# A new first stage, new visits to the caches and a re-dealt last norm in a one-layer inference step

## The chip, the cores and the metric

The kernel runs on one core of a Trainium2 chip. The core has TensorE (PE, matrix multiplies; PEld is its weight load), VectorE (DVE), ScalarE (ACT), GpSimd (POOL) and SyncE (SP), which here only issues DMAs. Data lie in HBM, in the on-chip SBUF of 128 partitions, and in PSUM, which PE accumulates into and which DVE and ACT read. The metric is the device time in microseconds of one execution; the number compared is the median over several executions.

## The reference

One layer of a decoder trunk is computed for a prompt of 256 positions and for 8 samples of 4 new positions, together 288 tokens of width 2048, all in float32:

```python
z = x @ w_in                                   # h, Bg, Cg, q, k, v, g_a, g_b
ya = gate_b * causal_dwconv3(gate_c * h)       # mixer A
# mixer B: three head groups with windows (128, 512, 2048) and dilations (1, 4, 16),
# 4 heads of 128 each, ALiBi; the softmax is merged over the groups
mixed = sigmoid(g_a) * (ya @ w_branch_a) + sigmoid(g_b) * (yb @ w_branch_b)
x1 = layernorm(ALPHA * x + mixed @ w_out)
a, b = split(x1 @ w_up)
y = layernorm(ALPHA * x1 + (silu(causal_dwconv3(a)) * b) @ w_down)
```

The samples attend to cached keys and values (`cache_kv0`, `cache_kv1`, `cache_kv2`). Beside `y` the outputs are the window buffers: new keys and values, the caches with the new rows behind them, and the last rows entering the two convolutions. So the cache tiles that the attention reads are also written out again.

## The kernel before, in words

Tokens are columns and features are rows. x lies as 16 chunks (`KD`) of 128 features by 288 tokens. Each float32 operand of a large product is split in two: a copy rounded to the type `fp32r` (ACT, `whi`, `xh`) and the remainder (DVE, `wlo`, `xl`). A block of 128 output features takes, for each of its 16 chunks, three matmuls of 288 columns: `whi` by `xh`, `whi` by `xl`, `wlo` by `xh` (`mms`, L217 to L219). `product` (L196) takes a prepared weight block, calls `prepare` for the next (one load of 1 MB on SP's queue, L176, and its split in halves by ACT and DVE, L223), and then issues the 48 matmuls. PE runs one product after another: 36 for q, k and v, 48 for mixer A, 64 for the two gated branches, 16 for `w_out`, then 88 for `w_up` and 48 for `w_down` in three parts.

**First stage.** While the data land, PE runs `N_WARM` matmuls on zeros (L235). The first three blocks of `w_in` are worked on together. `FIRST` (L69) cuts the 16 chunks into six pieces: 2, 2, 2, 2, 4 and 4 chunks. For each piece x comes by one DMA (L253; the first four from ACT's queue, the last two from SP's), two weight blocks by a second (`dd`, L254) and the third block by a third (`wst`, L255). ACT casts and DVE subtracts piece by piece: x (`xh`, `xl`), the two blocks (`yal`, `cache`), the third block (`whi`, `wlo`). PE (L285) goes by piece, then by the three terms, then by chunk and block. x lies in SBUF as two halves of 144 tokens per chunk with `HX` = 160 elements from half to half; one matmul reads the halves alternately. In the compiled program the DMAs of ACT's and SP's queues use eight completion semaphores in turn, so that a DMA is issued only when the eighth before it has landed.

**Visits to the caches.** The sample attention reads 18 key tiles and 18 value tiles of 1 MB. It is a generator, `sample_steps`, which `product` advances at a fixed rate (`N_STEP` of `N_STEP_BLOCKS`, L201 to L205), from the first k product on. At each step PE visits two tiles (L450 for keys, L506 for values, eight float32 matmuls of 512 columns a visit, or 32 of 128 in group 0), and `fetch_two` (L418) then loads the next two tiles into two `cache` buffers and writes them out again. Before each group DVE masks the queries, or the weights, by sample in one pass of 1024 columns (`by_batch`, L412). So there are 9 visits for the keys and 9 for the values. `prompt_attention` (L340 to L398) is spread over products in the same way.

**Last norm.** The last `w_down` products end in `dd`; `finish_out` (L712) normalises it. PE sums the last parts into mean and mean square (L686, L687). DVE and ACT work out the variance and its inverse root, with one correction step on DVE (L736, L737) whose result `dev` lies in PSUM. Each of 16 chunks of `dd` then needs the mean subtracted, the factor multiplied and gain and bias applied. `NORM_DVE` lists the passes of DVE in order ("m" subtract, "r" multiply, with first chunk and count); POOL subtracts chunks 8 to 15 (`MEAN_POOL`) and multiplies 12 to 15 (`OUT_POOL`), for which ACT copies the factor to SBUF (`r_pool`, L738). ACT applies gain and bias (L747) to chunks 0 to 7 and 12 to 15, DVE (L745) to 8 to 11. Six stores go out in `OUT_ORDER` (L748).

The order on each engine follows program order and explicit pairs (`behind`, `tc.issue_after`); a scheduler places the rest.

Of the kernel before, what the change touches and what calls it, by code (L numbers as in the profile page):

```python
# [11 lines left out]
F32R = mybir.dt.float32r  # L12
# [5 lines left out]
P = 128  # L18
# [11 lines left out]
HX = 160  # L30
# [23 lines left out]
C_M0 = C_TM + NT  # L54
C_M1 = C_M0 + NG * P
# [31 lines left out]
def layer_kernel(ctx: ExitStack, tc: tile.TileContext, ins, outs):  # L87
# [40 lines left out]
    spent = [0]  # L128
# [42 lines left out]
    def prepare():  # L171
        src, nk = next(w_left, (None, 0))
        if nk == 0:
            return
        st = sb(wp, [P, KD, P], "wst")
        d = sp.dma_start(st[:, :nk, :], src.rearrange("p (k c) -> p k c", c=P))  # L176
# [19 lines left out]
    def product(x):  # L196

        w = w_ready.pop(0)
        if not w_ready:
            prepare()  # L200
        if steps_on[0]:  # L201
            spent[0] += N_STEP
            while spent[0] >= N_STEP_BLOCKS:
                spent[0] -= N_STEP_BLOCKS
                next(steps, None)  # L205
# [31 lines left out]

    xh = sb(big, [P, KD, 2, HX], "xh", F32R)
    xl = sb(big, [P, KD, 2, HX], "xl", F32R)
# [6 lines left out]
    w_two_lo = [sb(wk, [P, 2, HK, P], "cache", F32R, bufs=2) for _ in range(2)]  # L246
# [4 lines left out]
    for k0, n, queue in FIRST:  # L251
        k = slice(k0, k0 + n)
        (act if queue == "act" else sp).dma_start(xs[:, k], x_in[:, k])  # L253
        sp.dma_start(w_two[:, :, k], w_in_two[:, :, k])  # L254
        sp.dma_start(w_one[:, k], w_in_one[:, k])  # L255
    splits = []
    for k0, n, _ in FIRST:
        k = slice(k0, k0 + n)
        splits.append(split(xh[:, k, :, :H], xl[:, k, :, :H], xs[:, k].rearrange("p k (a h) -> p k h a", h=2)))
        h = slice(k0 % HK, k0 % HK + n)  # L260
        splits.append(split(w_two_hi[:, :, k], w_two_lo[k0 // HK][:, :, h], w_two[:, :, k]))
        splits.append(split(w_one_hi[k0 // HK][:, h], w_one_lo[k0 // HK][:, h], w_one[:, k]))
    for before, after in zip(splits, splits[1:]):
        for i in range(2):
            behind(after[i], before[i])
# [3 lines left out]
    def first_three():  # L269
# [10 lines left out]
        for k0, n, _ in FIRST:  # L280
            for term in range(3):
                for k in range(k0, k0 + n):
                    xk = x[term == 1][:, k].rearrange("p h a -> p a h")
                    for b in range(3):
                        i = pe.matmul(  # L285
                            o[b], first_w(term == 2, b, k), xk, start=k == 0 and term == 0, stop=k == KD - 1 and term == 2
                        )
                        if before is not None:
                            behind(i, before)
                        before = i  # L290
        return [t.rearrange("p a h -> p h a") for t in o]

    cst = sb(big, [P, C_M0], "cst")

# [106 lines left out]
    bmask = cst[:, C_BM : C_BM + NB * NS].rearrange("p (b r) -> p b r", b=NB)  # L401
    tmask = cst[:, C_TM : C_TM + NT]

    sw = sb(wk, [P, NH * NB * NS + 1152], "sw", bufs=1)
    sw_m = sw[:, : NH * NB * NS].rearrange("p (j b r) -> p j b r", j=NH, b=NB)
    sw2 = sw[:, NH * NB * NS :]

    def by_batch(src):

        m = sw_m  # L410
        shape = [P, NH, NB, NS]
        dve.tensor_tensor(m, src.unsqueeze(2).broadcast_to(shape), bmask.unsqueeze(1).broadcast_to(shape), ALU.mult)  # L412
        return m

    cache_left = iter([(which, n) for which in ("ck", "cv") for n in range(N_CT)])
    cache_tiles = []

    def fetch_two():  # L418

        for _ in range(2):  # L420
            which, n = next(cache_left, (None, 0))
            if which:
                t = sb(wk, [P, 2048], "cache", bufs=2)
                behind(sp.dma_start(t, ins[which][n]), w_load[0])
                sp.dma_start(outs["o_" + which][n], t)
# [9 lines left out]
    def sample_steps():  # L435
        fetch_two()
        yield
        row = []
        s = sw2[:, :SW]
        sbias = cst[:, C_SB : C_SB + SW]  # L440
        for g in range(NG):
            qm = by_batch(q_s[:, g])
            cols = P if g == 0 else NT * P
            p = sb(ps, [P, cols], "long", bufs=1)
            for b in range(NB):
                if g > 0 or b % 4 == 0:
                    c = cache_tiles.pop(0)
                o = (b % 4) * NH * P if g == 0 else 0
                for j in range(NH):
                    row.append(pe.matmul(  # L450
                        p[j * NS : (j + 1) * NS], qm[:, j, b, :], c[:, o + j * cols : o + (j + 1) * cols],
                        start=b == 0, stop=b == NB - 1,
                    ))
                if g == NG - 1 and b == NB - 1:
# [9 lines left out]
                if b == NB - 1 or (g > 0 and b % 2 == 1):  # L464
                    in_a_row(row)
                    row = []
                    fetch_two()
                    yield
            sg = s[:, g * P : (g + 1) * P]
            if g == 0:  # L470
                dve.tensor_tensor(sg, p, sbias[:, :P], ALU.add)
            else:
                pick_t(sg, p, sbias[:, g * P : (g + 1) * P])
        dve.tensor_tensor(s[:, NG * P :], pn, sbias[:, NG * P :], ALU.add)
        st = sb(wk, [P, 4], "st", bufs=4)
        dve.reduce_max(st[:, 0:1], s, AX.X)
        dve.tensor_scalar_mul(st[:, 1:2], st[:, 0:1], -SCALE)
        act.activation(s, s, AF.Exp, bias=st[:, 1:2], scale=SCALE, accum_out=st[:, 2:3])
        dve.reciprocal(st[:, 3:4], st[:, 2:3])
        dve.tensor_scalar_mul(s, s, st[:, 3:4])  # L480
        pt = att()
        for g in range(NG):
            pe.transpose(pt[:, g * P : (g + 1) * P], s[:, g * P : (g + 1) * P], ident)
        pt2 = att()
        pe.transpose(pt2[: NG * NS, :P], s[:, NG * P :], ident)
        sT = sw2[:, : NG * P].rearrange("p (g r) -> p g r", g=NG)
        act.copy(sT, pt[:, : NG * P].rearrange("p (g r) -> p g r", g=NG))
        sTn = sw2[: NG * NS, NG * P : NG * P + P]
        act.copy(sTn, pt2[: NG * NS, :P])
        vn = sw2[: NG * NS, NG * P + P : NG * P + P + NH * P].rearrange("p (j d) -> p j d", j=NH)  # L490
        pv = att()
        for j in range(NH):
# [528 lines left out]
```

## Time and profile before

| | |
|---|---|
| median of 3 runs | 1757.73 us (1757.28 to 1758.61) |
| profiled execution | 1758.0 us, its span 1756.2 us |
| PE busy in the span | 1738.8 us |
| DVE, ACT, POOL busy | 1006.7, 797.9, 243.7 us |
| bytes moved | 436.25 MB, mean 248 GB/s |

How to read it: times in the trace count from the span's first instruction. A busy share is an average over stages, so the stage decides what a change is worth; the chain of work that ended last tells which instruction each piece of time belongs to. Rows of matmuls overlap: one of 288 columns is shown with 286 ns, but they start 0.12 us apart. A row of the timeline gives start, duration, engine, line, operation, result and operands, a count where rows are merged, and in brackets the idle time before it and what ended it. "x18" behind a row means 18 instructions.

### The profile page before, as it was taken

The page shows a single profiled execution, that of the slowest core. Times are in us where ns is not written, and L with a number is a line of the kernel's source. Part 1 is how long each engine was busy: PE and PEld are TensorE (multiplying, and loading weights), DVE is VectorE, ACT ScalarE, POOL GpSimd, SP SyncE. Part 2 cuts the span into 40 slices and gives each one's busy share as a digit, 9 for nine tenths or more (in the row PEclk, how much of TensorE's full clock was granted, in tenths as well). Part 3 has the DMA queues.
Part 4 walks back from the last instruction along what each step waited for, and adds up shares of the span by engine and source line. Part 5 has one row for each costly group of instructions (what it writes and reads, how often), then busy time and mean ns, then how long its engine had stood idle before and what let it go on. Part 6 is the DMA issues. An engine that isn't in the chain of part 4 may idle for free.

```text
span 1756.2 us, 33518 instructions
## 1 busy us (share of the span) xinstructions
PE 1738.8 (99%) x14257; PEld 1710.7 (97%) x14257; DVE 1006.7 (57%) x1278; ACT 797.9 (45%) x1142; POOL 243.7 (14%) x404
## 2 busy tenths in 40 slices
PE   9999999999999999999999999999999999999996
PEld 9999999999999999999999999999999999999996
DVE  5444445555555444455588888765555555555554
ACT  5444444334434333344455655544454443345444
POOL 0000000000000000001165333300011110011165
PEclk9999999999999999999999999999999999999998
DMA  9477787787787877477766656566666666666662
GB/s 330 170 287 274 274 307 283 280 326 282 299 322 272 319 300 264 150 252 264 259 251 224 231 219 231 224 226 230 224 232 221 235 218 238 219 236 217 225 217 102
DMA packets 61350, 436.25 MB, mean 248 GB/s; under 512 B 7312, under 2 KB 9360, under 8 KB 17296
## 3 DMA queue, kind: packets, MB, share of 16 engines
q1 hardware_dynamic: 59472, 429.40, 66.4%
q10 hardware_dynamic: 1728, 4.72, 0.7%
q8 instruction: 111, 1.82, 0.4%
q14 instruction: 39, 0.32, 0.1%
HBM read 389.89 MB, written 94.53 MB: 276 GB/s over the span
## 4 chain that ended last, share of the span: by engine, by line
PE 99%; DMA 0%; DVE 0%; ACT 0%; SPq 0%; ACTq 0%; issue 0%; DVEq 0%
PE acc L217 32%; PE acc L219 31%; PE acc L218 31%; PE long L506 1%; PE long L450 1%; PE acc L285 1%; DMA dd<-in_w_in 0%; PE att L391 0%; ACT yah L747 0%; DVE dd L723 0%; PE att L351 0%; PE acc L383 0%; PE att L349 0%; PE att L374 0%; PE att L687 0%; PE att L686 0%
## 5 line engine op out<-in xcount | busy, mean ns | idle before, releaser
L223 DVE TENSOR_TENSOR wlo<-wst,whi 128x1024 fp32r<-128x1024 f32 (+2 forms) x584 | 709.1, 1215 | 613.1 <-ACT whi L223 607.6
L223 ACT CAST whi<-wst 128x1024 fp32r<-128x1024 f32 (+2 forms) x584 | 593.3, 1017 | 888.0 <-PE acc L218 777.7
L217 PE MATMUL acc<-xh,whi 128*128 128x288 f32 (+1 forms) x3216 | 922.8, 287 | 0.0
L218 PE MATMUL acc<-xl,whi 128*128 128x288 f32 (+1 forms) x3216 | 920.4, 286 | 0.0
L219 PE MATMUL acc<-xh,wlo 128*128 128x288 f32 (+1 forms) x3216 | 920.3, 286 | 0.0
L217 PEld LDWEIGHTS acc<-xh,whi 128*128 128x128 f32 x3216 | 607.8, 189 | 10.3 <-ACT h L606 2.5
L218 PEld LDWEIGHTS acc<-xl,whi 128*128 128x128 f32 x3216 | 607.8, 189 | 0.2 <-issue 0.2
L219 PEld LDWEIGHTS acc<-xh,wlo 128*128 128x128 f32 x3216 | 607.8, 189 | 0.0
L217 PE MATMUL acc<-yah,whi 128*128 128x288 f32 x1216 | 347.9, 286 | 0.0
L219 PE MATMUL acc<-yah,wlo 128*128 128x288 f32 x1216 | 347.7, 286 | 0.0
L218 PE MATMUL acc<-yal,whi 128*128 128x288 f32 x1216 | 347.7, 286 | 0.0
L217 PEld LDWEIGHTS acc<-yah,whi 128*128 128x128 f32 x1216 | 229.7, 189 | 2.5 <-ACT h L628 2.5
L218 PEld LDWEIGHTS acc<-yal,whi 128*128 128x128 f32 x1216 | 229.8, 189 | 0.0
L219 PEld LDWEIGHTS acc<-yah,wlo 128*128 128x128 f32 x1216 | 229.8, 189 | 0.0
L584 POOL COPY qk_s<-u 128x2 f32<-128x2 f32 x44 | 38.1, 866 | 571.4 <-ACT u L798 448.6
L572 DVE SCALAR_TENSOR_TENSOR cy<-u,prm,cy 128x304 f32<-128x304 f32 x120 | 72.4, 603 | 3.8 <-ACT cy L570 0.7
L643 POOL TENSOR_TENSOR ya<-ya,dd 128x288 f32<-128x288 f32 x16 | 13.6, 850 | 306.0 <-DVE ya L642 306.0
L595 DVE TENSOR_TENSOR ya<-cy,acc 128x256 f32<-128x256 f32 x88 | 23.5, 310 | 33.8 <-PE acc L219 33.7
L223 ACT CAST yah<-ya 128x288 fp32r<-128x288 f32 x76 | 32.7, 430 | 16.6 <-DVE ya L600 8.5
L584 POOL COPY cm<-u 128x2 f32<-128x2 f32 x16 | 3.0, 185 | 256.5 <-DVE u L611 256.5
L677 POOL TENSOR_TENSOR cache<-cache,dd 128x288 f32<-128x288 f32 x29 | 29.1, 1002 | 52.6 <-DVE dd L763 33.6
L223 DVE TENSOR_TENSOR yal<-ya,yah 128x288 fp32r<-128x288 f32 x76 | 34.9, 460 | 1.3 <-ACT yah L223 1.1
(174 smaller groups left out, 830.2 us busy)
## 6 DMA issues: line engine op xcount, KB each, us to landing
wst<-in_w_in SPq DMA_DIRECT2D x113, 1024.0 KB, 6.2
wst<-in_w_up SPq DMA_DIRECT2D x88, 1024.0 KB, 4.8
wst<-in_w_down SPq DMA_DIRECT2D x32, 1024.0 KB, 4.8
cache<-in_ck SPq DMA_DIRECT2D x18, 1024.0 KB, 6.4
out_o_ck<-cache SPq DMA_DIRECT2D x18, 1024.0 KB, 10.1
cache<-in_cv SPq DMA_DIRECT2D x18, 1024.0 KB, 5.6
out_o_cv<-cache SPq DMA_DIRECT2D x18, 1024.0 KB, 9.4
wst<-in_w_a SPq DMA_DIRECT2D x16, 1024.0 KB, 6.1
```

What stands on the lines that cost most here:

```text
L217: pe.matmul(out, hi[:, c, :], xh_k, start=k == 0, stop=False)
L218: pe.matmul(out, hi[:, c, :], xl_k, start=False, stop=False)
L219: last_mm[0] = pe.matmul(out, lo[:, c, :], xh_k, start=False, stop=k == nk - 1)
L223: return act.copy(hi, src), dve.tensor_tensor(lo, src, f32(hi), ALU.subtract)
L285: i = pe.matmul(o[b], first_w(term == 2, b, k), xk, start=k == 0 and term == 0, stop=k == KD - 1 and term == 2)
L450: row.append(pe.matmul(p[j * NS : (j + 1) * NS], qm[:, j, b, :], c[:, o + j * cols : o + (j + 1) * cols], start=b == 0, stop=b == NB - 1,))
L506: row.append(pe.matmul(p[j * NS : (j + 1) * NS], sm[:, j, b, :], c[:, o + j * cols : o + (j + 1) * cols], start=b == 0 and g < 2, stop=b = ...
L572: dve.scalar_tensor_tensor(y, u[:, i : i + YW], prm[:, w0 + i : w0 + i + 1], y, ALU.mult, ALU.add)
L584: pool.tensor_copy(dst[:, 0:2], u[:, SEQ : SEQ + 2])
L595: dve.tensor_tensor(a, b, c, ALU.mult)
L643: pool.tensor_tensor(m, m, ma[:, i], ALU.add)
L677: pool.tensor_tensor(self.s1, self.s1, d, ALU.add)
```

## The change

In the first stage all pieces have two chunks (`N_PIECE`), eight in number. ACT issues x of piece 0, then a copy of two columns that brings its table load forward, then x of piece 1; x of the other six pieces is issued by SP. The first x piece is cast chunk by chunk, and the first piece of the two blocks is copied by DVE, chunk by chunk. PE takes blocks 0 and 1 before block 2 within each term. `HX` becomes `2 * HG + 2` = 292 per chunk, with both halves in one row, 145 elements from half to half. The warm-up has 17 matmuls. The load of the block after the first three comes in two halves.

The caches get three buffers, and a visit takes three tiles (`N_VISIT`) every eighth product (`APART`); `fetch` does one DMA per product, a load or the store of the tile loaded before. Steps start in the q products. Masks are made per sample, 128 columns a pass, two products ahead of the visit, from one zero-padded row of the constants; the constants therefore come in three DMAs. The score and output tiles of some groups move to `att` buffers, and the scratch moves into the tile `dd`.

In the last norm DVE multiplies chunk 0 alone, then pairs; POOL subtracts chunks 3 to 12 and multiplies 11 and 12 only; ACT's copy of the factor stands after DVE's pass over chunks 5 and 6, beside the pass over 13 to 15 which reads the mean; DVE applies gain and bias to 12 to 15; there are seven stores.

```diff
-HX = 160
+HX = 2 * HG + 2
-FIRST = ((0, 2, "act"), (2, 2, "act"), (4, 2, "act"), (6, 2, "act"), (8, 4, "sp"), (12, 4, "sp"))
-N_WARM = 18
-N_STEP = N_CT + 2
-N_STEP_BLOCKS = 2 * NG * NH + 5 * KD - 3
-NORM_DVE = ("m", 0, 3), ("r", 0, 3), ("m", 3, 3), ("r", 3, 3), ("m", 6, 2), ("r", 6, 2), ("r", 8, 2), ("r", 10, 2)
-MEAN_POOL = (8, 2), (10, 2), (12, 2), (14, 2)
-OUT_POOL = (12, 2), (14, 2)
-GB_DVE = (8, 9, 10, 11)
-OUT_ORDER = (0, 3), (3, 3), (6, 2), (8, 4), (12, 2), (14, 2)
+N_PIECE = 2
+N_WARM = 17
+N_VISIT = 3
+APART = 8
+NORM_DVE = (
+    ("m", 0, 3), ("n", 0, 0), ("r", 0, 1), ("r", 1, 2), ("r", 3, 2), ("r", 5, 2), ("c", 0, 0), ("m", 13, 3), ("r", 7, 2),
+    ("r", 9, 2), ("r", 13, 3), ("g", 13, 3), ("g", 12, 1),
+)
+MEAN_POOL = (3, 2), (5, 2), (7, 2), (9, 2), (11, 2)
+OUT_POOL = ((11, 2),)
+OUT_ORDER = (0, 2), (2, 2), (4, 2), (6, 2), (8, 2), (13, 3), (10, 3)
...
@@ prepare
+        for k0 in range(0, nk, HK if loads[0] == 1 else nk):
+            k = slice(k0, k0 + (HK if loads[0] == 1 else nk))
+            d = sp.dma_start(st[:, k, :], src[:, k])
@@ first stage
-    xh = sb(big, [P, KD, 2, HX], "xh", F32R)
+    xh = sb(big, [P, KD, HX], "xh", F32R)[:, :, : 2 * HG].rearrange("p k (h a) -> p k h a", h=2)
...
+    for k0 in range(0, KD, N_PIECE):
+        k = slice(k0, k0 + N_PIECE)
+        if k0 == N_PIECE:
+            i_table = act.copy(sb(wk, [P, 2], "wgb", bufs=2), f32(zero[:, :2]))
+        i_x = (act if k0 <= N_PIECE else sp).dma_start(xs[:, k], x_in[:, k])
+        if k0 == N_PIECE:
+            behind(i_x, i_table)
         sp.dma_start(w_two[:, :, k], w_in_two[:, :, k])
         sp.dma_start(w_one[:, k], w_in_one[:, k])
...
+        for n, (hi, lo, src) in enumerate(parts):
+            if k0 or n == 2:
+                casts.append(act.copy(hi, src))
+            else:
+                for c in range(N_PIECE):
+                    e = (slice(None),) * (1 + n) + (slice(c, c + 1),)
+                    if n == 0:
+                        casts.append(act.copy(hi[e], src[e]))
+                    else:
+                        rests.append(dve.tensor_copy(hi[e], src[e]))
+        rests += [dve.tensor_tensor(lo, src, f32(hi), ALU.subtract) for hi, lo, src in parts]
...
+                for blocks in ((0, 1), (2,)):
+                    for k in range(k0, k0 + N_PIECE):
...
@@ caches
+    def by_batch(n, src, b):
+        m = bmask[:, (NB - 1 - b) * NT : (NB - 1 - b) * NT + NS]
+        dve.tensor_tensor(sw_m[:, n], src, m.unsqueeze(1).broadcast_to([P, NH, NS]), ALU.mult)
...
-    def fetch_two():
-        for _ in range(2):
+    def fetch():
+        if to_store:
+            sp.dma_start(*to_store.pop())
+        elif len(cache_tiles) < N_VISIT:
             which, n = next(cache_left, (None, 0))
             if which:
-                t = sb(wk, [P, 2048], "cache", bufs=2)
+                t = sb(wk, [P, 2048], "cache", bufs=3)
                 behind(sp.dma_start(t, ins[which][n]), w_load[0])
-                sp.dma_start(outs["o_" + which][n], t)
+                to_store.append((outs["o_" + which][n], t))
                 cache_tiles.append(t)
...
+        for values in range(2):
+            for first in range(0, N_CT, N_VISIT):
+                here = held[first : first + N_VISIT]
+                for n in range(APART):
+                    fetch()
+                    if values and first == 0 and n == 3:
+                        transposed()
+                    if n == APART - 2:
...
+                    yield
...
@@ last norm
             for what, k0, n in NORM_DVE:
+                if what == "c":
+                    act.copy(r_pool, dev)
+                    for p0, pn in OUT_POOL:
+                        by_token(pool, p0, pn, r_pool, ALU.mult)
+                    continue
                 with tc.issue_after(before.ins):
-                    before = by_token(dve, k0, n, *((mean, ALU.subtract) if what == "m" else (dev, ALU.mult)))
-                if n_op == 0:
-                    with tc.issue_after(before.ins):
+                    if what == "n":
                         dve.scalar_tensor_tensor(t, t, -0.5, v, ALU.mult, ALU.mult)
                         before = dve.scalar_tensor_tensor(dev, t, 1.5, r, ALU.add, ALU.mult)
-                    act.copy(r_pool, dev)
+                    elif what == "g":
+                        for i in range(k0, k0 + n):
+                            before = g_b(i)
+                    else:
+                        before = by_token(dve, k0, n, *((mean, ALU.subtract) if what == "m" else (dev, ALU.mult)))
```

More of the change, by code (lines that the diff above doesn't have):

```diff
@@ L201, in product @@
         if steps_on[0]:
[L202 to L205, printed above, removed]
+            next(steps, None)
         o = acc(x[0].shape[-1])
@@ L435, in sample_steps @@
     def sample_steps():
-        fetch_two()
-        yield
-        row = []
         s = sw2[:, :SW]
         sbias = cst[:, C_SB : C_SB + SW]
[L441 to L446, printed above, removed]
-                    c = cache_tiles.pop(0)
[L448 to L454, printed above, removed]
+        sT = sw2[:, : NG * P].rearrange("p (g r) -> p g r", g=NG)
@@ L463, in sample_steps @@
                     ]
[L464 to L475, printed above, removed]
@@ L486, in sample_steps @@
[L486 to L492, printed above, removed]
-            pe.transpose(pv[: NG * NS, j * P : (j + 1) * P], v_s[:, j].rearrange("p g r -> p (g r)"), ident)
-        act.copy(vn, pv[: NG * NS].rearrange("p (j d) -> p j d", j=NH))
@@ L527, in sample_steps @@
+                in_a_row(row)
+                for g in rest_of:
+                    if not values:
+                        scored(g, p[g])
+                    elif g == 0:
+                        act.copy(o_sb, p[0])
+                    elif g == NG - 1:
+                        pick_t(o_sb, p[g], o_sb)
+            if not values:
+                softmax()
+        yield
         po = att(P)
         pe.transpose(po, o_sb, ident)
-        oT = sw[:, :P]
+        oT = sw_m[:, 0].rearrange("p j r -> p (j r)")
```

204 lines of the change are left out of this document (111 added, 93 removed).

## The prediction

> **What bounds the kernel now.** I read the page first, then the trace's windows by stage, then the chain of waits at the start, around one visit to the caches and at the end. The page's second line is the span; below it are three windows, whose columns are length, then busy time and rows of PE, PEld, DVE, ACT and POOL, the granted clock, the DMA share and GB/s.
>
> ```profile
> span 1756.2 us, 33518 instructions
> ```
>
> ```profile
> 0.00:26.00 26.00, 23.78 (x165) 22.70 (x166) 15.41 (x21) 15.66 (x22) 1.35 (x9) 1.00 0.96 335
> 26.00:1739.00 1713.00, 1713.00 (x14087) 1686.78 (x14086) 981.37 (x1242) 773.36 (x1103) 234.11 (x389) 1.00 0.68 248
> 1739.00:1757.00 18.00, 2.00 (x9) 1.18 (x7) 9.91 (x16) 8.88 (x18) 8.21 (x6) 0.63 0.33 131
> ```
>
> From 26 to 1739 us PE is never idle at full clock, while DVE and ACT have a third to a half to spare. There only fewer or cheaper PE instructions can help. Outside it, the first 26 us wait for data and the last 17 us for the norm. The change touches all three places, so I price each.
>
> **The first stage.** Rows of the timeline, then the chain, then windows and one DMA wait:
>
> ```profile
> 0.73 1.89 ACTq L253 DMA_DIRECT2D yah<-in_x  x4
> 1.22 4.69 PE L235 MATMUL acc<-cy 128*128 128x288 f32 x18 [1.22 <-DVE cy L232]
> 2.65 1.28 ACT L223 ACT_TABLE_LOAD   x1 [2.65 <-issue]
> 5.05 0.72 ACT L223 CAST xh<-yah 128x576 fp32r<-128x576 f32 x1 [1.12 <-DMA yah<-in_x]
> 5.68 0.61 ACT L223 CAST yal<-dd 128x512 fp32r<-128x512 f32 x1
> 5.80 0.76 DVE L223 TENSOR_TENSOR xl<-yah,xh 128x576 fp32r<-128x576 f32 x1 [4.64 <-ACT xh L223]
> 6.35 0.51 PE L285 MATMUL acc<-xh,yal 128*128 128x288 f32 x2 [0.44 <-ACT yal L223]
> 6.66 0.40 ACT L223 CAST whi<-wst 128x256 fp32r<-128x256 f32 x1 [0.37 <-DMA wst<-in_w_in]
> 22.91 2.00 ACT L223 CAST whi<-wst 128x1024 fp32r<-128x1024 f32 x2 [1.59 <-DMA wst<-in_w_in]
> ```
>
> ```profile
> 8.97 0.63 ACT yal L223
> ...
> 9.64 11.73 PE acc L285 x92
> ...
> 25.81 0.12 PE acc L217
> ```
>
> ```profile
> 0.00:4.00 4.00, 2.78 (x11) 2.79 (x12) 0.30 (x1) 1.28 (x1) 0.62 (x8) 1.00 0.52 83
> 4.00:12.00 8.00, 7.00 (x44) 6.22 (x44) 4.86 (x9) 5.31 (x11) 0.00 (x0) 1.00 1.07 373
> 14.00:20.00 6.00, 6.00 (x51) 5.93 (x50) 4.54 (x4) 3.30 (x5) 0.00 (x0) 1.00 1.05 414
> ```
>
> ```profile
> yah<-in_x ACTq DMA_DIRECT2D x4, 288.0 KB, 5.6
> ```
>
> The reader is to see that x lands at 5.05, PE starts at 6.35, does one piece, and stands until the second piece of the two blocks lands at 8.97 and is cast. From 9.64 the other 126 of 144 matmuls end at 25.81. The later rows give a matmul's pace.
>
> ```profile
> 505.36 1.85 PE long L506 x16
> 507.21 0.32 PE acc L217
> 507.53 0.12 PE acc L218
> ...
> 511.45 0.12 PE acc L217
> ```
>
> From 507.53 to 511.45 are 32 starts, 0.1225 us each. So 144 matmuls are 17.6 us, and the stage takes 25.81 - 6.35 = 19.5.
>
> *Data.* A piece of two chunks is 288 + 256 + 128 KB, 0.688 MB. Before, four x pieces (1.18 MB) stood in ACT's queue beside the first weights. Now only two do, and SP sends the rest piece by piece. By the windows 0.33 MB have come by 4 us and 3.31 MB by 12, then 414 GB/s. At that pace piece 1 is in at 5.0 us, piece 2 at 6.8, piece 3 at 8.7, and piece 8 at 17.3.
>
> *Casts.* Per piece ACT needs 0.72 + 0.61 + 0.40 = 1.73 us; DVE's passes take no more (4.86 busy against ACT's 5.31 in the window from 4 to 12). PE needs 18 x 0.1225 = 2.2, so neither falls behind once a piece is in.
>
> *PE.* It can start when one chunk of x (half of 0.72) is cast and DVE has copied one chunk of weights: about 5.5. The 17 warm-up matmuls hold PE until about 5.65 (18 rows took 4.69 from 1.22). I take 5.6, and 0.4 of waiting inside the first piece (xl follows ACT's second chunk and a 0.76 pass), so it ends at 8.2. Piece 2, in at 6.8 and cast by 6.8 + 0.72 + 0.61 = 8.1, follows at once. The other 126 matmuls are 15.4 us: end 23.6 instead of 25.81, **2.2 us less**. Upper end: no wait inside the piece, 5.65 + 17.6 = 23.25, 2.6 less. Lower end: the first rival below, 0.4 less.
>
> What is late next is the fourth block. It was in at 22.91, for use at 25.81. It now comes as two halves behind 5.5 MB, the first at about 18.6. If it came no earlier than before (half of it some 1.3 us ahead of 22.91), its cast (1.0) and subtraction (1.2) would end at 23.8, 0.2 late. The table load ran in the gap before 5.05 at no cost. Now it stands ahead of x piece 1's issue. The three DMAs of constants and the split load add issue time of half a microsecond each on SP, which waits for landings anyway.
>
> [...] The trace shows the load at 1.28 us alone, and in the tail the next ACTIVATE begins 0.01 us after such a load ends:
>
> ```profile
> 1735.77 1.28 ACT L681 ACT_TABLE_LOAD   x1
> 1737.06 0.20 ACT L681 ACTIVATE cache<-cy 128x1 f32<-128x1 f32 x1
> ```
>
> [...]
>
> **The visits.** Around a visit PE's time from 505.36 to 507.53 is 2.17 us, 2.05 beside the one matmul in it. Group 0's value visit shows what more work in one visit costs:
>
> ```profile
> 447.10 1.88 PE long L506 x64
> 448.99 0.22 PE long L513 x8
> ```
>
> Eight rows added to a running visit took 0.22, so 64 are 1.76, and 0.12 of the 1.88 is entering. The matmul behind takes 0.32 instead of 0.12. So a visit costs 0.20 to 0.32 beside its rows. The rows stay the same in number; 18 visits become 12: 6 x 0.20 = 1.2 to 6 x 0.32 = 1.9, I take **1.6 less**. Nothing else of PE's 1713 us changes. Bound from the other side: no gain, if the cost goes with tiles.
>
> DVE's masks become 48 passes of 128 columns; the nearest row is a pass of that size:
>
> ```profile
> L471 DVE TENSOR_TENSOR sw<-long,cst 128x128 f32<-128x128 f32 x1 | 0.3, 280 | 0.0
> ```
>
> 48 x 0.28 = 13.4 us, less the six long passes that go, covered by DVE's 730 idle us and issued two products ahead of use; without cover it would be at most 9 x 0.28 = 2.5 us at one visit. SP's queue waits longer in front of the weight loads than anything else there:
>
> ```profile
> SPq L425 <- DMA cache<-in_ck: 50.8, 17, 6.8
> ```
>
> The columns are us in total, times, longest. Waits of up to 6.8 us never reached PE (1713.0 of 1713.0 busy). In the new order a store comes a product (48 x 0.1225 = 5.9 us) after its load, so that wait shrinks; the wait of a load for a visit remains, 12 times instead of 18. I cost both at nothing.
>
> **The last norm.**
>
> ```profile
> 1741.33 8.21 POOL L723 TENSOR_TENSOR dd<-dd,cache 128x576 f32<-128x576 f32 x6 [4.42 <-ACT cache L718]
> 1742.97 0.46 DVE L737 SCALAR_TENSOR_TENSOR long<-cache,acc 128x288 f32<-128x288 f32 x1
> 1743.47 0.40 ACT L738 COPY cache<-long 128x288 f32<-128x288 f32 x1 [1.02 <-DVE long L737]
> 1743.90 1.05 DVE L723 TENSOR_TENSOR dd<-dd,long 128x864 f32<-128x864 f32 x1 [0.47 <-ACT cache L738]
> 1747.04 4.83 ACT L747 ACTIVATE yah<-dd,prm 128x288 f32<-128x288 f32 x9 [0.35 <-DVE dd L723]
> 1747.70 2.08 DVE L723 TENSOR_TENSOR dd<-dd,long 128x576 f32<-128x576 f32 x3
> 1749.70 1.44 DVE L745 TENSOR_SCALAR yah<-dd,prm 128x288 f32<-128x288 f32 x4
> ```
>
> DVE stands 0.47 for ACT's copy, because both read `long`, and ACT's first gain follows a pass of 1.05. The last gain ends at 1747.04 + 4.83 = 1751.87. New order on DVE: chunk 0 from 1743.45, 0.46 as for the row of that size, to 1743.9; three pairs 2.08, to 1745.98; the mean over 13 to 15, 1.0, to 1746.97. On ACT: gain 0 at 1743.95; gains 1 to 4 from 1744.6 (first pair) at 4.83/9 = 0.54, to 1746.8; then the copy, 0.40, to 1747.2. DVE's next pair waits 0.2 for it. From 1747.2: two pairs 1.39, a triple 1.0, four gains 1.44: 1751.05. ACT: seven gains 3.76: 1750.95. POOL: six passes still end at 1741.33 + 8.21 = 1749.54, ahead of gain 11. So the last value is ready **0.8 us earlier**. The store behind it has 432 KB instead of 288; at 414 GB/s that is 0.4 more, so the lower end is 0.4. The upper is 1.1, if seven even stores leave less queued at the end.
>
> **Sum.** 2.2 + 1.6 + 0.8 = 4.6. The profiled execution took 1758.0 (span 1756.2 and 1.8 around it); 1758.0 - 4.6 = 1753.4. That execution is 0.3 above the median 1757.73, so a median of 1753.1.
>
> **The rivals.**
> *x piece 1 is late.* ACT issues it behind the table load, at about 2.7 instead of 1.2. Four such loads took 5.6 us to land: 8.3; then casts 0.72 + 0.61, PE at 9.7, end 9.7 + 15.6 = 25.4. The start gives 0.4: sum 2.8, 1754.9. For: before, x was already the DMA that ACT waited for. Against: those 5.6 us were four in the same queue, now two.
> *Visits cost by the tile.* No gain in the middle: 3.0 in all, 1754.7. For: entering shows only 0.12. Against: the 0.32 row behind every visit.
> *The other side: xh's new half stride.* 9648 matmuls read `xh` or `xl` in steps of 145 elements instead of 160.
>
> ```profile
> L217 PE MATMUL acc<-xh,whi 128*128 128x288 f32 (+1 forms) x3216 | 922.8, 287 | 0.0
> L217 PE MATMUL acc<-yah,whi 128*128 128x288 f32 x1216 | 347.9, 286 | 0.0
> ```
>
> 160 (`xh`) and 144 (`yah`) run alike, both even; no row shows an odd stride. It decides from 4.6 us / 9648 = 0.5 ns a matmul; at 1 ns it costs 9.6, total 1762.7.
>
> **How the numbers follow.** About 0.2% (3.5 us) is what a measurement of this kernel can tell from no change, so faster means below 1754.2. The forecast has 0.60, the late x 0.17, visits by the tile 0.13 (both end within 0.2%), the stride or another stall of PE in its full stretch 0.10, of which 0.08 ends slower. Of the forecast's own share 0.03 falls short of 3.5. So faster 0.57, same 0.35, slower 0.08. The ends together: 2.6 + 1.9 + 1.1 = 5.6 gives 1752.1, less the 0.3 between runs 1751.8; for the range I go to 1751.5. Above, both rivals together (0.4 + 0 + 0.8 = 1.2) give 1756.5; I stop at 1755.8, which holds each alone.
>
> **What would show it.** The fourth block's first matmul at about 23.6 (25.4 with a late x). Twelve visits, each followed by one 0.32 row. PE busy all the time between first stage and norm, with 0.1225 a matmul. ACT's first gain in the norm at 1.0 us after `dev` became 0.5 us. Wrong would be any idle PE in the middle, above all at loads behind a visit, or matmuls of `xh` slower than those of `yah`.

## The result

The changed kernel takes 1753.25 us (median of 12 runs, 1752.99 to 1753.96); the kernel before, measured beside it, takes 1757.32 us (12 runs, 1756.95 to 1758.61). The ratio is 0.9977, with a 95% interval of 0.997 to 0.9984. No run of the one reaches into the runs of the other, and the interval stays clear of 1, so the changed kernel is faster, by 0.23%. The prediction drew its line at 0.2%; the median lies beyond it, the interval reaches across it (0.9984). The forecast of 1753.1 us is 0.15 us away.

The profiled execution took 1753.35 us. First its page's span, then the windows by stage (length, busy time and rows of PE, PEld, DVE, ACT and POOL, granted clock, DMA share, GB/s), cut where the stages now end:

```profile
span 1751.6 us, 33565 instructions
```

```profile
0.00:24.00 24.00, 22.54 (x163) 22.15 (x164) 15.94 (x29) 16.81 (x30) 1.35 (x9) 1.00 0.97 335
24.00:1736.00 1712.00, 1712.00 (x14091) 1687.87 (x14091) 986.93 (x1285) 773.87 (x1104) 233.31 (x389) 1.00 0.68 249
1736.00:1752.00 16.00, 1.15 (x5) 0.54 (x4) 9.53 (x16) 8.67 (x18) 8.26 (x6) 0.60 0.38 147
```

The shape is the old one. PE has no idle time between the first stage and the norm, so what the middle gained is PE's own time. The start, from the timeline (start, duration, engine, line, operation, result and operands, idle time before and its cause):

```profile
0.73 0.45 ACTq L262 DMA_DIRECT2D yah<-in_x  x1
1.21 1.28 ACT L261 ACT_TABLE_LOAD   x1 [1.21 <-PEq L1056]
1.27 0.45 ACTq L262 DMA_DIRECT2D yah<-in_x  x1
2.51 0.19 ACT L261 COPY wgb<-cy 128x2 f32<-128x2 f32 x1
5.15 0.81 ACT L284 CAST xh<-yah 128x288 fp32r<-128x288 f32 x2 [2.45 <-DMA yah<-in_x]
5.34 0.50 DVE L286 CAST yal<-dd 128x256 fp32r<-128x256 f32 x2 [4.17 <-DMA dd<-in_w_in]
5.78 0.74 PE L311 MATMUL acc<-xh,yal 128*128 128x288 f32 x4 [0.24 <-DVE yal L286]
...
8.38 0.65 PE L311 MATMUL acc<-xh,yal 128*128 128x288 f32 x4
```

x's second piece is issued at 1.27, inside the table load (1.21 to 2.49). PE starts at 5.78 instead of 6.35, and the second piece follows at 8.38 with no wait, where the kernel before stood until 9.64. The chain of work that ended last (start, duration, piece) gives the stage's ends and one visit:

```profile
0.74 4.58 DMA dd<-in_w_in
5.34 0.31 DVE yal L286
...
5.78 18.20 PE acc L311 x144
23.98 0.12 PE acc L223
...
149.64 2.71 PE long L529 x24
152.35 0.32 PE acc L223
...
1735.21 0.97 PE att L726 x4
```

By the chain the fourth block begins at 23.98 (before 25.81), the norm's first matmul at 1735.21 (before 1739.06). The chain lets a piece begin where the one ahead of it ends: the timeline has these matmuls 0.16 to 0.17 us earlier (23.81 and 1735.05, before 25.64 and 1738.90), since the rows of matmuls overlap. All starts of blocks below are the chain's. The tail's timeline:

```profile
1739.62 2.45 DVE L763 TENSOR_TENSOR dd<-dd,long 128x288 f32<-128x288 f32 x4
1740.11 2.90 ACT L773 ACTIVATE yah<-dd,prm 128x288 f32<-128x288 f32 x5 [1.50 <-DVE dd L763]
1742.89 0.38 ACT L778 COPY cache<-long 128x288 f32<-128x288 f32 x1
1743.16 3.81 ACT L773 ACTIVATE yah<-dd,prm 128x288 f32<-128x288 f32 x7
1743.38 2.38 DVE L763 TENSOR_TENSOR dd<-dd,long 128x576 f32<-128x576 f32 x3 [0.34 <-ACT cache L778]
1745.80 1.45 DVE L772 TENSOR_SCALAR yah<-dd,prm 128x288 f32<-128x288 f32 x4
```

The last value is ready at 1745.80 + 1.45 = 1747.25, 4.35 us ahead of the span's end; before it was 1751.87, 4.33 ahead. A DVE wait for ACT's copy is still there, 0.34 instead of 0.47.

So three differences make up the whole, with *start* for the time to the fourth block's first matmul, *middle* from there to the norm's first matmul, and *tail* from there to the span's end (all in us):

| kernel | start | middle | tail | span | median of runs |
|---|---|---|---|---|---|
| before | 25.81 | 1713.25 | 17.14 | 1756.2 | 1757.32 |
| changed | 23.98 | 1711.23 | 16.39 | 1751.6 | 1753.25 |
| difference | -1.83 | -2.02 | -0.75 | -4.60 | -4.07 |

The median moved half a microsecond less than the profiled pair, because the profiled execution of the kernel before (1758.0) was 0.7 above the later median of its runs, and that of the changed kernel only 0.1.

### The profile page after: what moved, and what is told of

Read it like the earlier page. It is cut to its first block, busy times and chain, and to the rows that moved or that the text cites. A ratio compares the mean times of both kernels' runs of the same rounds, so it can differ in the third digit from the quotient of the medians.

```text
span 1751.6 us, 33565 instructions
## 1 busy us (share of the span) xinstructions
PE 1735.7 (99%) x14256; PEld 1710.6 (98%) x14256; DVE 1012.4 (58%) x1329; ACT 799.4 (46%) x1149; POOL 242.9 (14%) x404
## 4 chain that ended last, share of the span: by engine, by line
PE 99%; DVE 0%; DMA 0%; ACT 0%; issue 0%; DVEq 0%
PE acc L223 32%; PE acc L224 31%; PE acc L225 31%; PE long L529 1%; PE acc L311 1%; PE att L529 1%; PE att L418 0%; DMA dd<-in_w_in 0%; DVE dd L763 0%; PE att L378 0%; PE acc L410 0%; PE att L376 0%; ACT yah L773 0%; PE att L401 0%; DVE yah L772 0%; PE att L727 0%
## 5 line engine op out<-in xcount | busy, mean ns | idle before, releaser
L229 DVE TENSOR_TENSOR wlo<-wst,whi 128x1024 fp32r<-128x1024 f32 (+1 forms) x578 | 706.5, 1223 | 595.9 <-ACT whi L229 592.5
L229 ACT CAST whi<-wst 128x1024 fp32r<-128x1024 f32 (+1 forms) x578 | 590.6, 1022 | 879.9 <-PE acc L224 775.8
```

Source lines behind the costliest of these rows:

```text
L229: return act.copy(hi, src), dve.tensor_tensor(lo, src, f32(hi), ALU.subtract)
```

## The experiments

Each experiment alters the changed kernel in one place, or takes one of its parts back, and none leaves out any of the work. Each is judged by the three numbers above; where there were several runs, the median stands too.

**How a visit is priced: two tiles and one tile a visit.** The 36 tiles are read in 18 visits, or in 36, instead of 12.

```diff
-N_VISIT = 3
-APART = 8
+N_VISIT = 2      # the other kernel: 1
+APART = 5        # the other kernel: 2
```

With one tile a visit, three smaller things differ too: the visits start two products later, the transposition of the attention weights moves to another step, and the scores of the third head group lie in `long`.

> The changed kernel with visits of two tiles every fifth product instead of three every eighth: 18 visits instead of 12, all else as changed. Theory (each visit costs PE 0.33 us beside its rows: 0.13 on entering and 0.20 behind it): 6 x 0.33 = 2.0 us more between the first product's matmul and the norm, so that stretch goes from 1711.2 back to about 1713.2 and the time to about 1755.2. Rival (the cost goes with the tiles, and the middle gained for another reason): the stretch stays within 0.3 us of 1711.2.

> One tile a visit every second product, 36 visits, started at the first k product. Theory (cost by the visit): 24 x 0.33 = 7.9 us more than the changed kernel, stretch about 1719.1, time about 1761.2, slower than the kernel before by 3.8. Rival (by the tile): stretch 1711.2, time 1753.3. A second rival, that visits so close together make PE wait for cache loads, would show idle PE in front of the visits on top.

Two rows of the chain of the kernel with 18 visits, then two of that with 36: the fourth block's first matmul and the norm's.

```profile
23.75 0.12 PE acc L223
...
1737.03 0.97 PE att L726 x4
```

```profile
24.31 0.12 PE acc L223
...
1743.58 0.97 PE att L726 x4
```

The middle is 1713.28 us with 18 visits and 1719.27 with 36, against 1711.23 with 12. Six visits more cost 2.05 us, 24 more 8.04: 0.34 us each, both times to within 0.01. PE waits for nothing in either middle, so the second rival, waits for cache loads, is out. With 18 visits the middle is that of the kernel before (1713.25), so the number of visits accounts for all of its gain; the masks, the single fetches and the new buffers give and take nothing there in sum. The medians are 1755.67 (1755.09 to 1755.88; ratio to before 0.999, 0.9981 to 1.0) and 1761.59 (1761.23 to 1761.88; 1.0024, 1.0014 to 1.0033): with one tile a visit the change as a whole would have been a loss.

**The first stage and the norm taken back, one at a time.** One kernel has the old `FIRST`, the old queues and order of casts and the load of the fourth block in one piece, PE's old order of blocks included, on the new layout of x; the other has the old `NORM_DVE`, pools and six stores.

```diff
-N_PIECE = 2
-N_WARM = 17
+FIRST = ((0, 2, "act"), (2, 2, "act"), (4, 2, "act"), (6, 2, "act"), (8, 4, "sp"), (12, 4, "sp"))
+N_WARM = 18
```

```diff
-OUT_ORDER = (0, 2), (2, 2), (4, 2), (6, 2), (8, 2), (13, 3), (10, 3)
+NORM_DVE = ("m", 0, 3), ("r", 0, 3), ("m", 3, 3), ("r", 3, 3), ("m", 6, 2), ("r", 6, 2), ("r", 8, 2), ("r", 10, 2)
+OUT_ORDER = (0, 3), (3, 3), (6, 2), (8, 4), (12, 2), (14, 2)
```

> The changed kernel with the first stage of the kernel before (six pieces, four x loads on ACT's queue, all casts on ACT, 18 warm-up matmuls, blocks in the old order, one load for the fourth block). Theory (the parts add): the fourth block's first matmul back from 23.98 to 25.8, everything later shifted by 1.8 and no longer, time about 1755.1. Rival (part of the first stage's gain is also given back later, or some of it came from elsewhere): the stretch from there to the norm differs from 1711.2 by over 0.3.

> The changed kernel with the last norm of the kernel before. Theory: from the norm's first matmul to the end of the span 17.1 us instead of 16.4, time about 1754.0. Rival (the tail's gain comes from the stages ahead, not from the deal): 16.4.

The fourth block's and the norm's first matmul in the chain, first with the old first stage, then with the old norm:

```profile
25.63 0.12 PE acc L223
...
1736.86 0.97 PE att L705 x4
```

```profile
26.24 0.12 PE acc L220
...
1737.48 0.97 PE att L723 x4
```

| kernel | start | middle | tail | median of runs |
|---|---|---|---|---|
| old first stage | 25.63 | 1711.23 | 16.34 | 1754.93 (1754.21 to 1755.14) |
| old norm | 26.24 | 1711.24 | 17.2 | 1754.45 (1753.76 to 1756.45) |

The old first stage costs 1.65 us at the start (1.68 by the medians), the old norm 0.8 in the tail, and neither moves the middle. By the medians the old norm costs 1.20, and 18 and 36 visits cost 2.42 and 8.34: 0.3 to 0.4 more each than the stage that was altered. Where that rest lies no profile shows. The old norm's start of 26.24 belongs to neither theory. Its rows in the timeline:

```profile
6.26 1.30 PE L308 MATMUL acc<-xh,yal 128*128 128x288 f32 x4 [0.59 <-DVE yal L283]
...
9.27 1.17 PE L308 MATMUL acc<-xh,cache 128*128 128x288 f32 x4
...
10.64 0.66 PE L308 MATMUL acc<-xh,yal 128*128 128x288 f32 x4
```

Its first stage is the changed kernel's, yet until about 10.5 us four matmuls take 1.17 to 1.30 us instead of 0.65, with 0.24 us between starts instead of 0.12. PE had stood 0.59 us between the warm-up and the data. The profiled execution was the slowest of its ten runs (1756.45; the others lie at 1753.76 to 1754.52). Two experiments below take this up.

**Which queue x comes in.** Four x pieces in ACT's queue, as before the change, instead of two.

```diff
-        i_x = (act if k0 <= N_PIECE else sp).dma_start(xs[:, k], x_in[:, k])
+        i_x = (act if k0 < 4 * N_PIECE else sp).dma_start(xs[:, k], x_in[:, k])
```

> Four of the eight x pieces go to ACT's queue instead of two; the rest is the changed kernel. My step: two x pieces more at ACT's head compete with the first weight pieces, so the second weight piece lands about 0.6 us later and the first matmuls of piece 2 wait: the fourth block's first matmul at 25.0 to 25.4 instead of 23.98. Rival: which queue an x piece is in does not matter as long as PE's backlog covers it: 23.98 within 0.3. Middle (fourth block to norm) 1711.2 and tail 16.4 in both.

A row of its timeline and one of its chain:

```profile
9.42 0.76 PE L311 MATMUL acc<-xh,yal 128*128 128x288 f32 x4 [0.51 <-ACT yal L278]
```

```profile
25.12 0.12 PE acc L223
```

The wait for the second weight piece (`yal`) is back, and the start is 25.12, 1.14 later; middle and tail are 1711.24 and 16.3. So most of the first stage's gain comes from sending x's third and fourth piece behind the weights, and not from the earlier first matmul, which this kernel has too (5.75). The other 0.69 against the kernel before is shared: the second piece starts at 9.42 instead of 9.64, and from there to the fourth block PE needs 15.70 us instead of 16.17, with eight small pieces instead of six.

**Does the first matmul's start set the end?** The first x and weight piece are cast whole by ACT, with no share for DVE.

```diff
-            if k0 or n == 2:
+            if True:
                 casts.append(act.copy(hi, src))
```

> In the first piece ACT casts the upper part whole, as in the later pieces, instead of sharing it with VectorE; the rest is the changed kernel. My step (the first matmul's start sets the end, since PE then runs 144 matmuls without a wait): the first matmul moves from 5.78 to 6.2 to 6.5 and the fourth block's first matmul with it, to 24.4 to 24.7. Rival (the weights' arrival sets the end, the start is slack): it stays at 23.98 within 0.2. If the row of the first matmuls shows 0.24 us each beyond the first 1 us, the idle time ahead of them has cost the clock, and the end is at 25 to 26.

One row of its timeline and one of its chain:

```profile
5.97 0.76 PE L311 MATMUL acc<-xh,yal 128*128 128x288 f32 x4 [0.30 <-ACT yal L278]
```

```profile
24.15 0.12 PE acc L223
```

The first matmul comes 0.19 later and the fourth block 0.17 later. From the one to the other are 18.18 us here, 18.20 in the changed kernel and 18.19 in that with 18 visits, so there the start sets the end. It does not always: six other profiles of this first stage have 18.31 to 18.72, because PE then waited for the third block's weights or ran slow for a while (below). The size was missed: I had put the first matmul at 6.2 or later, but here x landed at 4.67, some 0.5 earlier than in the changed kernel's profile (5.15). From x's landing to the first matmul are 1.30 us here and 0.63 there, so an estimate from these two is that the fine casting saves up to 0.7 us when x lands last. The two ends themselves can't show it, since they scatter by as much (below).

**xh's odd half stride.** 146 floats from half to half instead of 145.

```diff
-    xh = sb(big, [P, KD, HX], "xh", F32R)[:, :, : 2 * HG].rearrange("p k (h a) -> p k h a", h=2)
+    xh = sb(big, [P, KD, HX], "xh", F32R).rearrange("p k (h a) -> p k h a", h=2)   # and xl
```

> The two halves of xh and xl stand 146 floats apart instead of 145, the row of 292 stays; the rest is the changed kernel. My reading: the stride of the matmul's moving operand costs nothing, so the middle (fourth block's first matmul to the norm's first) stays at 1711.2 within 0.3. Rival (an odd stride costs each matmul 0.5 ns or more): the middle gets 6 us or more shorter. If it gets longer, the even stride is what costs.

Two rows of its chain:

```profile
24.38 0.12 PE acc L223
...
1735.63 0.97 PE att L726 x4
```

The middle is 1735.63 - 24.38 = 1711.25 against 1711.23, one profile of each. The odd stride costs nothing.

**ACT's copy of the factor two chunks earlier.** It stands after DVE's pass over chunks 3 and 4 instead of 5 and 6, and DVE's pass over 13 to 15 moves with it, so that it still runs beside the copy.

```diff
-... ("r", 3, 2), ("r", 5, 2), ("c", 0, 0), ("m", 13, 3), ("r", 7, 2),
+... ("r", 3, 2), ("c", 0, 0), ("m", 13, 3), ("r", 5, 2), ("r", 7, 2),
```

> VectorE reads the three tiles' squares one step later: after only two gain steps of ACT the copy is put in, and VectorE's later step has moved behind another. My step (the 0.34 us for which VectorE stands before its second group of squares comes from ACT's copy being late, and that group is on the way to the end): the wait is gone and the tail is 16.0 to 16.2 instead of 16.39. Rival (the tail is set by the last gains and the stores, and VectorE has slack): 16.39 within 0.1, with the wait gone. Start and middle as in the changed kernel.

DVE's rows in its tail:

```profile
1741.56 1.04 DVE L763 TENSOR_TENSOR dd<-dd,att 128x864 f32<-128x864 f32 x1
1742.55 3.05 DVE L763 TENSOR_TENSOR dd<-dd,long 128x576 f32<-128x576 f32 x4
1745.64 1.61 DVE L772 TENSOR_SCALAR yah<-dd,prm 128x288 f32<-128x288 f32 x4
```

No wait is left in front of the second row, and the tail is 16.15 instead of 16.39. (The expectation's "squares" are these passes that multiply by the factor.) The 0.34 us wait was on the path, and 0.24 of it comes back.

**A longer and a shorter warm-up.** Thirteen matmuls on zeros, which leaves PE standing longer ahead of the data, and twenty, which leaves no gap; twenty also together with the earlier copy.

```diff
-N_WARM = 17
+N_WARM = 13      # the other kernels: 20
```

> Thirteen warm-up matmuls instead of seventeen; the rest is the changed kernel. Theory (an idle stretch of PE ahead of the first data lets its pace fall back: 0.24 us a matmul instead of 0.12 for about 3.5 us): warm-up ends at about 4.6, PE stands about 1 us, the first 16 or so matmuls take 0.24 each, and the fourth block's first matmul is at 25.5 to 26.5, as in the kernel with the old norm (26.24), against 23.75 to 24.4 in the others. Rival (the slow pace there was a chance of that run and an idle stretch costs nothing): 23.7 to 24.4. Middle 1711.2 and tail 16.4 in both.

> Twenty warm-up matmuls instead of seventeen; the rest is the changed kernel. Theory (the idle stretch sets the pace): PE runs from the warm-up into the first data without standing, all 144 matmuls of the first three blocks go at 0.12 us, the fourth block's first matmul is at 23.6 to 24.2 and the runs lie closer together than the changed kernel's; median 1752.7 to 1753.4. Rival (three matmuls more only push the first data's matmuls back, by 0.12 to 0.24 each): the first starts at 6.1 to 6.4, the fourth block at 24.3 to 24.7, median 1753.6 to 1754.0.

> The earlier copy of the last norm and twenty warm-up matmuls together. If both help: tail 16.15, middle 1711.2, fourth block's first matmul at 23.6 to 24.2, median 1752.5 to 1753.1, below the changed kernel's 1753.25. If the longer warm-up only costs: tail 16.15 and start 24.3 to 24.7, median 1753.3 to 1753.8.

With thirteen, the timeline of the start, a window of it (its last three columns are granted clock, DMA share and GB/s) and the chain's row of the fourth block:

```profile
5.68 1.30 PE L311 MATMUL acc<-xh,yal 128*128 128x288 f32 x4 [0.97 <-ACT xh L284]
...
8.94 1.16 PE L311 MATMUL acc<-xh,cache 128*128 128x288 f32 x4
...
10.38 0.73 PE L311 MATMUL acc<-xh,yal 128*128 128x288 f32 x4
```

```profile
8.00:10.00 2.00, 2.00 (x10) 2.00 (x10) 2.00 (x5) 1.92 (x4) 0.00 (x0) 1.00 1.09 366
```

```profile
26.05 0.12 PE acc L223
```

PE stands 0.97 us, and then runs at 0.24 us a matmul until about 10.4, for 18 matmuls, nearly as the theory said (its 3.5 us stands in no run: from the first data on the slow pace lasted 4.7 us here and 4.2 in the kernel with the old norm). The start is 26.05, 2.07 later than in the changed kernel, with the first matmul 0.10 earlier. The window shows ten matmuls in 2 us where the changed kernel has nineteen. Its column of the granted clock has 1.00 in both; the last section says why that column can't be used here.

With twenty, rows of the timeline:

```profile
5.90 0.65 PE L311 MATMUL acc<-xh,yal 128*128 128x288 f32 x4
6.79 0.51 PE L311 MATMUL acc<-xh,whi 128*128 128x288 f32 x2 [0.24 <-ACT whi L278]
```

Here the first data run at full pace from the first matmul, and the start is 24.21 (24.13 in the combined kernel). But now PE waits for the third block's first weights (`whi`), which landed at 6.31 in this execution. The median is 1753.59 (1753.12 to 1753.91), no better than with seventeen, and 24.21 and 1753.59 lie just above what the theory said, while the first matmul at 5.90 lies ahead of what the rival said; combined with the earlier copy it is 1753.31 (1752.82 to 1753.56), where the changed kernel has 1753.25. The forecast for the combined kernel, 1752.5 to 1753.1, is missed by its median: the tail gave its 0.24 (16.14), the start did not give anything. No version here beats the changed kernel by more than can be measured.

**Without the copy that calls the table load early.**

```diff
-            i_table = act.copy(sb(wk, [P, 2], "wgb", bufs=2), f32(zero[:, :2]))
-        if k0 == N_PIECE:
-            behind(i_x, i_table)
```

> ACT's small copy is left out, with which the table load was called ahead of x's second piece; the first cast now calls it. Theory (a load that stands beside waiting for the first data costs nothing, and it does not hold ACT's DMA issue): fourth block's first matmul at 23.7 to 24.4. Rival (the load goes ahead of whatever first needs it and so moves into the way of the first casts): xh's first casts start 1.3 us later and the fourth block with them, at 25.0 to 25.6.

ACT's rows at its start:

```profile
1.69 1.28 ACT L282 ACT_TABLE_LOAD   x1 [1.69 <-PEq L1054]
4.92 0.81 ACT L282 CAST xh<-yah 128x288 fp32r<-128x288 f32 x2 [1.95 <-DMA yah<-in_x]
```

The load now belongs to the first cast, but it runs as soon as ACT's DMA issues are out, and ACT then waits 1.95 us for x all the same. The start is 24.40, at the upper end of what this first stage shows; its first four matmuls took 1.30 us, the slow pace again for about a microsecond. The early load buys nothing that shows in one profile.

**How far the start scatters.** Nine profiles share the DMA order of the changed kernel's first stage, its own among them, and show PE standing 0.5 us at most at a time in it: their starts are 23.75, 23.98, 24.13, 24.15, 24.21, 24.22, 24.31, 24.38 and 24.40. (Left out are the two with longer stands, 26.05 and 26.24.) What the chain of the start goes back to differs from one execution to the next: the first two blocks' weights in the changed kernel's profile, the third block's in those with 24.13, 24.21, 24.22 and 24.38. In those with 24.31 and 24.40 the first matmuls ran at the slow pace until about 7 us. Five of the nine have the changed kernel's first stage with nothing altered but the visits, the norm or the stride of x (23.75, 23.98, 24.22, 24.31, 24.38). So some 0.6 us of the start is a matter of the execution, and differences below that aren't read from single ones.

## Why the prediction was right

*The bound.* Start and tail wait for data and for the norm, and PE is full between. This held.

*The first stage: 2.2 us forecast, 1.83 measured (1.65 against the kernel with the old first stage).* The mechanism is the one described: with x's third and fourth piece out of ACT's queue, piece 2 follows piece 1 at once, which the kernel with four pieces on ACT undoes. The first piece took 2.60 us from 5.78 to 8.38, the 2.2 + 0.4 of the working, and 0.3 of the 0.4 lies where it was put: the first matmul with `xl` starts at 6.80, behind DVE's pass for it (5.99 to 6.75), where six matmuls at full pace would have been over at 6.52. The other 126 start 0.1225 us apart, as forecast. Two things made the 2.2 too large. The first matmul came at 5.78, not 5.6: the working let the warm-up's end set it, but the chain shows the first two blocks' weights, landed at 5.32 and copied by DVE. And the working set a sum of starts, 23.6, against the 25.81 of the chain, which is the end of the last matmul ahead; the fourth block's first matmul starts at 25.64 there, and at 23.81 in the changed kernel. Like with like, the forecast was 2.0. The fourth block, which was named as late next, was not late: PE's only waits in the changed kernel are those ahead of the warm-up and of the first data.

*The visits: 1.6 us forecast, 2.02 measured, beyond the upper end of 1.9.* The prediction took 0.20 to 0.32 for a visit beside its rows and chose between. But 0.20 was the slower matmul behind the visit alone, and 0.12 was entering it; both are paid at each visit, so the two terms had to be added, not bracketed. The upper end, 0.32, was the sum; the runs show 0.34. The rows agree: a visit of 24 matmuls takes 2.71 us in the changed kernel and one of 16 took 1.85 before, so eight are 0.86, and 0.13 is left over in both for entering; the matmul behind takes 0.32 in both, 0.20 more than another. That is 0.33 a visit.

*DVE's masks and SP's queue: nothing forecast, nothing measured.* The row that the prediction shows for SP's queue is that of the stores (L425), which wait for their loads to land, and not that of the weight loads of which its sentence speaks (L176, 1265.6 us in all). The waits of the stores went the other way than was said (columns: us in total, times, longest). First the row of the values of the kernel before, beside the row of its keys in the prediction, then both rows of the changed kernel:

```profile
SPq L425 <- DMA cache<-in_cv: 47.7, 18, 3.7
```

```profile
SPq L449 <- DMA cache<-in_cv: 68.9, 18, 6.3
SPq L449 <- DMA cache<-in_ck: 64.0, 17, 6.7
```

The stores' waits for their loads were to shrink. They are 132.9 us in all, against 50.8 + 47.7 before. A load of a tile now takes 8.3 us (keys) and 7.1 us (values) from issue to landing, by the medians of the page, where it took 6.4 and 5.6, so the 5.9 us of a product between load and store do not cover it. The longest wait is 6.7, and none of it reached PE, which is what the zero rested on.

*The last norm: 0.8 forecast, 0.75 measured.* By the working the last value was to be ready 1751.05 - 1739.06 = 11.99 us after the norm's first matmul; it was 1747.25 - 1735.21 = 12.04. The wait of DVE for the copy was 0.34 instead of 0.2. The 0.4 us for a larger last store, which made the lower end, did not come: 4.35 us from the last value to the end, against 4.33. The kernel with the old norm gives the 0.8 back, and that with the earlier copy shows that DVE's wait for it was on the path.

*The sum.* The 4.6 us came out exactly in the profiled pair, but that is luck: 0.4 too much in the first stage and 0.4 too little at the visits cancel. That 1753.25 lies so near 1753.1 is luck as well. By the medians the gain is 4.07, half a microsecond less than forecast; the forecast started from a median of 1757.73 over three runs, and twelve runs gave 1757.32. All three places gained by the mechanism named, each within its stated ends but for the visits, which gained more.

*The rivals.* The late x piece fell with its premise: ACT's queue issued x's second piece at 1.27, while the table load ran (1.21 to 2.49). That a load on ACT holds up ACT's DMA issues was taken from program order, and the trace shows that it does not. (Its sum is off by 0.1: 9.7 + 15.6 is 25.3, not 25.4.) The load held ACT for its own 1.28 us and little more: the copy begins at 2.51, 0.02 us after the load's 1.21 + 1.28, and each of the four later loads of the changed kernel begins 0.02 us after the ACT instruction ahead of it and is followed by the next within 0.02 us. The visits priced by tile fell with the two kernels above: the same 36 tiles cost 8.04 us more in 36 visits. The odd stride fell with the even one.

## What to carry to other kernels

Where PE is full, look for what it pays at each switch to another kind of matmul: here the price per switch was the time to enter plus the slower instruction behind, added (0.13 + 0.20 us), whatever the number of rows. In a start that waits for data, the order in which the queues bring the second piece was worth more than the first instruction's time (1.14 us of 1.83). A warm-up that ended 0.97 us ahead of the data cost 2.07 us, in one profile; one that reached into the data gained nothing over one that stopped 0.24 us short. And when a forecast sets a time against a row of the chain, make sure that both are starts, or both ends.

## What the runs showed of the hardware beyond that

*PE's slow start.* The pace of 0.24 us a matmul ends at a different time in each execution, though the warm-up always begins at 1.22: 17 warm-up matmuls took 3.93 us in the kernel with two tiles a visit and 4.45 us in that with the old norm. After PE had stood 0.97 and 0.59 us the slow pace lasted until about 10.4 and 10.5.

The granted clock of the windows, 1.00 throughout, doesn't show it, because these windows lie ahead of the trace's first record of the clock and are counted as full. The trace keeps the times at which the granted clock changed. The first record is a grant of the full clock, at 6.26 us in the kernel before and at 5.26 in the changed one. Until then the matmuls start 0.24 us apart, but for the first (0.40). Behind it they start 0.12 to 0.23 apart beside the waits, and 0.12 from 7.35 and 7.03 to the end of the piece. The grant lasts until after the last matmul: until 1743.64 with the last matmul at 1740.60, and until 1739.23 with the last at 1736.75. In the changed kernel the stand of 0.24 us came after the grant, and the slow pace did not come back behind it.

For the other kernels the rows of PE's timelines give the pace: four matmuls that start 0.24 us apart take 1.16 to 1.30 us, four at 0.12 take 0.65 (all in us, the last column estimated from the rows):

| kernel | warm-up | PE's stand ahead of the first data | row of the first data | slow pace until about |
|---|---|---|---|---|
| two tiles a visit | 17 in 3.93 | 0.41 | 4 in 0.73 | inside the warm-up |
| changed | 17 in 4.32 | 0.24 | 4 in 0.74 | inside the warm-up |
| before | 18 in 4.69 | 0.44 | 2 in 0.51 | the warm-up's end |
| old first stage | 18 in 4.69 | 0.43 | 2 in 0.80 | 7 |
| one tile a visit | 17 in 4.45 | none | 4 in 1.30 | 7 |
| thirteen warm-up matmuls | 13 in 3.49 | 0.97 | 4 in 1.30 | 10.4 |
| old norm | 17 in 4.45 | 0.59 | 4 in 1.30 | 10.5 |

In the other seven PE stood 0.45 us at most ahead of the first data, and the slow pace was over by 7.0. So in the twelve profiles with a stand of 0.45 us or less it ended by about 7, and in the two with 0.59 and 0.97 us it lasted until after 10. What ends it, and what decides between a stand of 0.45 and one of 0.59, no run shows.

Each kernel was profiled once, so how often a stand of 0.59 us goes with so long a slow pace is open; nine of the ten runs of the kernel with the old norm were 1.9 us or more shorter than the profiled one.
